# Three of the seven low parts of each residual factor made by GpSimd, in a one-core decoder layer

## The chip, the cores and the metric

The kernel runs on one core of a Trainium2 chip. The metric is the device time of one execution in microseconds; three runs of the kernel before gave 2371.24, 2372.51 and 2374.86 us, and the median, 2372.51 us, is its time. A core has a matrix engine (TensorE, PE in the rows), a vector engine (VectorE, DVE), a scalar engine (ScalarE, ACT), GpSimd (POOL) and SyncE (SP), whose queue issues nearly all transfers here. Each engine works through its own instructions in the order of the program and waits on semaphores where it needs another engine's result.

## The reference

One decoder layer on 512 tokens of width 2048, in float32. What matters here is the three matrix products behind the mixing heads, and what lies between them:

```python
x = x + jnp.concatenate([a_out, r_out], axis=-1) @ w_o[i]
h2 = rms_norm(x, g_ffn[i])
x = x + (jax.nn.silu(h2 @ w_gate[i]) * (h2 @ w_up[i])) @ w_down[i]
gate = jax.nn.sigmoid(rms_norm(x, g_ple[i]) @ w_ple_gate[i] + b_ple_gate[i])
x = x + (p[i] @ w_ple_proj[i]) * gate
```

Twice, a sum with the residual `x` becomes the left side of the next product: after `w_o` (for the gate and up products) and after `w_down` (for `w_ple_gate`). The factor of the norm that belongs to a token is applied behind the product, so the sum can be turned into factors as it comes, 512 columns at a time.

## The kernel before

Every product in float32 precision is made of three matrix products in a rounded format: an operand is split into a high part `H`, its rounded copy made by ScalarE, and a low part `L = source - H`, made by VectorE (`split`, lines 51 to 58). `mm3` multiplies high by high, high by low, low by high.

On top of that, most products run as seven block products in place of eight (a Strassen scheme with 512x512 quarters), named P1 to P7 and run in the order 1, 5, 6, 3, 7, 2, 4. The left side needs seven factors: `a0` and `a1` are two 128x512 chunks of the transposed sum, four of the factors are differences of their halves (`s1` to `s4`), three are halves themselves. `factors` (line 173) makes them: for each product, in that order, the subtraction where there is one, then the split, each on a tile of 128x256:

```python
made = {"1": a0[:, lo], "5": s1, "6": s2, "3": s4, "7": s3, "2": a1[:, lo], "4": a1[:, hi]}
for p in ORDER:
    if p in first:
        first[p]()
    H, L, end = sink(p)
    split(H, L, made[p])
    end()
```

The weights go through the same: each step of a stage (a `Group`: seven products of three or four weight units each) loads a weight tile of 128x1024 (`raw`, line 223), adds a second one to it on VectorE where the product wants a sum (line 81), splits it into `wh` (ScalarE, line 54) and `wl` (VectorE, line 55), and multiplies. `wh` and `wl` have three buffers each.

The sums become factors in `residual` (line 346). When the four token blocks of 512 columns are done, it calls `to_factors` twice (`u` = 0 and 1). TensorE transposes two chunks, ScalarE copies them out of PSUM with the gain of the norm into `a0` and `a1` (tile name `A`), and `factors` follows. There are two groups of columns (`n`), two halves of each (`nh`) and two calls (`u`), so eight calls after `w_o` and eight after `w_down`, in pairs. The buffers that the calls share are few, all from one pool: two for `A`, two for the differences (`t`, of which one holds `s1` and `s2`, the other `s3` and `s4`), four for the factors that are stored to memory first (`o`, line 191; the store is line 194). In the first group of columns all seven factors are stored and loaded again later (`s`, line 206); in the second one they are written straight into the tile `s` that the next stage reads, but for P4 of the first pair. `A` is also the scratch tile of the squares that ScalarE sums for the norm (line 365).

In this part of the program the order on each engine is the outcome of a scheduler that runs over the recorded operations (it reckons when each engine would come to them); TensorE's and the weight loads' program order is not pinned here. SyncE's one queue holds the stores of the factors, the loads of weights and the loads of the old residual, in one line. GpSimd has had little to do: it raises to the power -1/2 (line 84) and issues 16 stores (line 925).

Of the kernel before, what the change touches and what calls it, by code (L numbers as in the profile page):

```python
# [10 lines left out]
F32 = mybir.dt.float32  # L11
# [3 lines left out]
ALU = mybir.AluOpType  # L15
# [18 lines left out]
def layer_kernel(ctx, tc, x, xT, pT, g_mix, wqk, w_vg, qk_norm, g_ret, w_ow, g_ffn,  # L34
                 w_gu, w_dn, g_ple, w_pl, b_pg, w_pp,
                 ident_c, rope_c, ropeT_c, decay_c, mask_c, out):
    nc = tc.nc
# [10 lines left out]
    dram = ctx.enter_context(tc.tile_pool(name="dram", bufs=1, space=bass.MemoryType.DRAM))  # L48


    def split(H, L, src, scale=None):

        if scale is None:
            return (nc.scalar.activation(H, src, AF.Copy),  # L54
                    nc.vector.tensor_tensor(L, src, H.bitcast(F32), op=ALU.subtract))  # L55
        return (nc.scalar.activation(H, src, AF.Copy, scale=scale),
                nc.vector.scalar_tensor_tensor(L, src, scale, H.bitcast(F32),
                                               op0=ALU.mult, op1=ALU.subtract))
# [18 lines left out]
    def sub(o, a, b):  # L77
        nc.vector.tensor_tensor(o, a, b, op=ALU.subtract)  # L78
# [91 lines left out]
    def ev_tile(tag, bufs=2, shape=(P, T), name=None, dt=F32):  # L170
        return pools["ev"].tile(list(shape), dt, name=name or tag, tag=tag, bufs=bufs)

    def factors(a0, a1, sink):

        lo, hi = slice(0, 256), slice(256, 512)
        t = [ev_tile("t", 2, (P, 2, 256)) for _ in range(2)]
        s1, s2, s3, s4 = t[0][:, 0], t[0][:, 1], t[1][:, 0], t[1][:, 1]
        made = {"1": a0[:, lo], "5": s1, "6": s2, "3": s4, "7": s3, "2": a1[:, lo], "4": a1[:, hi]}
        first = {"5": lambda: sub(s1, a0[:, hi], a1[:, hi]), "6": lambda: sub(s2, a0[:, lo], s1),
                 "3": lambda: sub(s4, a1[:, lo], s2), "7": lambda: sub(s3, a1[:, hi], s2)}  # L180
        for p in ORDER:
            if p in first:
                first[p]()
            H, L, end = sink(p)
            split(H, L, made[p])
            end()

    def into(tiles, k):
# [22 lines left out]
    class Group:  # L211
# [36 lines left out]
        def extract(self, p, u):  # L248
            wh = wq.tile([P, 2, T], F32R, name="wh", tag="wh")
            wl = wq.tile([P, 2, T], F32R, name="wl", tag="wl")  # L250
            parts = split(wh, wl, self.raw[SOURCE[p], u])
            self.w[p, u] = wh, wl
            if p == "4":
                self.load_next("11", u)
            elif p == "7":
                self.load_next("12", u)
            self.ready(p, u)
            return parts
# [67 lines left out]
    def chunk_of(get, k):  # L326

        tp = tp_p.tile([P, T], F32, name="tp", tag="tp")
        for b in range(NB):
            transpose(tp[:, b * P:(b + 1) * P], get(b)[:, k * P:(k + 1) * P])  # L330
        return tp

    def to_factors(get, k0, sink, gain=None):

        tps = [chunk_of(get, k) for k in (k0, k0 + 1)]
        a1 = ev_tile("A")
        if gain is None:
            nc.scalar.activation(a1, tps[1], AF.Copy)
            factors(tps[0], a1, sink)
        else:  # L340
            a0 = ev_tile("A")
            nc.scalar.activation(a0, tps[0], AF.Copy, scale=gain(k0))
            nc.scalar.activation(a1, tps[1], AF.Copy, scale=gain(k0 + 1))
            factors(a0, a1, sink)

    def residual(n, i, units, old, new, turn):

# [7 lines left out]
        def finish(th, nh, b, part, t):  # L355
            tb = 2 * th + b
            s = 2 * n + nh
            o = t if (th, nh) == (0, 0) else part
            plus(o, part, t)
            later(1, lambda: nc.sync.dma_start(new(tb, s), o))  # L360
            if turn is None:
                return
            j, gain, where, tiles = turn
            sq = ev_tile("A", name="sq")
            nc.scalar.activation(sq, o, AF.Square, accum_out=ssq[j][:, tb, s:s + 1])
            outs[tb, nh] = o
            if len([k for k in outs if k[1] == nh]) < NB:
                return
            for u in range(2):
                k = 4 * n + 2 * nh + u  # L370
                sink = spill(where, k)
                if n == 1:
                    direct = into(tiles, k)
                    sink = (lambda p, a=spill(where, k - 2), b=direct: a(p) if p == "4" else b(p)) if nh else direct
                wait = 1 + 2 * u if n == 0 else units - 2 + u if nh else 1 + u
                later(wait, lambda u=u, sink=sink: to_factors(
                    lambda b: outs[b, nh], 2 * u, sink, lambda c: gain[:, 4 * s + c:4 * s + c + 1]))
            if n == 1 and nh == 0:
                rstd_of(ssq[j], rstd[j])
                if j == 2:  # L380
                    nc.vector.tensor_scalar(minus, rstd[j], -1.0, None, op0=ALU.mult)
# [30 lines left out]
    class Plain:  # L412
# [16 lines left out]
        def extract(self, p, u):  # L429
            self.w[u] = [wq.tile([P, 2, T], F32R, name=n, tag=n) for n in ("wh", "wl")]  # L430
            if u:
                return split(*self.w[u], self.raw[u])
            for c in range(2):
                split(*(w[:, c] for w in self.w[u]), self.raw[u][:, c])
# [426 lines left out]
    def mixed(i, made):  # L861
        spilled = spill(s_mix, i, 0)
        direct = into(s_o, i)
        assert (not s_o) == (i < 2 * NPAIR - 2)
        factors(*made, lambda p: (direct if p in s_o else spilled)(p))
# [98 lines left out]
    def swiglu(j):  # L964
        kg = min(j // 4, 2)
        act = {}

        def finish(th, nh, b, part, _):
            tb = 2 * th + b
            if nh == 1:  # L970
                act[tb] = part
                return
            r = rstd[1][:, tb:tb + 1]
            s = ev_tile("g", 4) if th == 0 else part
            nc.scalar.activation(s, part, AF.Silu, scale=r)
            a = act[tb]
            nc.vector.scalar_tensor_tensor(a, a, r, s, op0=ALU.mult, op1=ALU.mult)
            if tb == 3:
                for u in range(2):
                    sink = spill(s_a[kg], 2 * (j - 4 * kg) + u)  # L980
                    later(1 + 2 * u, lambda u=u, sink=sink: to_factors(lambda b: act[b], 2 * u, sink))
        return evacuate(finish)
# [132 lines left out]
```

## Time and profile before

| | |
|---|---|
| median of three runs | 2372.51 us (2371.24 to 2374.86) |
| the profiled execution | 2372.15 us, its span 2370.3 us |
| TensorE matmul busy | 2319.2 us (98%) |
| VectorE busy | 1943.6 us (82%), 2626 instructions |
| ScalarE busy | 1198.1 us (51%) |
| GpSimd busy | 59.0 us (2%), 47 instructions |
| granted TensorE clock, mean | 0.996 of full speed |

The span runs from the first instruction to the last, and 1.85 us of the execution lie outside it. TensorE is busy nearly all the time, so its idle time, some 51 us, and the time in which its clock is below full speed, are what other engines can cost. A busy share tells little by itself: the rows below look at the two places where sums become factors, 790 to 925 us and 2118 to 2236 us of the span. A row of the timeline gives start, duration, engine, line, operation, output and inputs, and in brackets how long the engine had idled before it and what ended that. VectorE's durations overlap a little: an instruction of 1.23 us that is followed at once by another is followed after some 1.14 us.

### The profile page before, as it was taken

The page shows a single profiled execution, that of the slowest core. Times are in us where ns is not written, and L with a number is a line of the kernel's source. Part 1 is how long each engine was busy: PE and PEld are TensorE (multiplying, and loading weights), DVE is VectorE, ACT ScalarE, POOL GpSimd, SP SyncE. Part 2 cuts the span into 40 slices and gives each one's busy share as a digit, 9 for nine tenths or more (in the row PEclk, how much of TensorE's full clock was granted, in tenths as well). Part 3 has the DMA queues.
Part 4 walks back from the last instruction along what each step waited for, and adds up shares of the span by engine and source line. Part 5 has one row for each costly group of instructions (what it writes and reads, how often), then busy time and mean ns, then how long its engine had stood idle before and what let it go on. Part 6 is the DMA issues. An engine that isn't in the chain of part 4 may idle for free.

```text
span 2370.3 us, 29145 instructions
## 1 busy us (share of the span) xinstructions
PE 2319.2 (98%) x10480; PEld 1900.2 (80%) x10480; DVE 1943.6 (82%) x2626; ACT 1198.1 (51%) x1791; POOL 59.0 (2%) x47
## 2 busy tenths in 40 slices
PE   9999999999999999999999999999999999999898
PEld 7888878888877877888888888888878878887677
DVE  8888586766667998888988898888888878789997
ACT  7644454444455565544554455444544434356553
POOL 0000011100010002000000000000000000000000
PEclk9999999999999999999999999999999999999999
DMA  6634734445666694346434643465577756857663
GB/s 237 236 130 162 232 104 127 131 147 179 200 219 259 218 359 153 109 155 200 154 113 146 200 160 120 138 196 166 195 318 253 291 224 214 344 196 268 245 197 124
DMA packets 166096, 463.59 MB, mean 196 GB/s; under 512 B 18496, under 2 KB 31168, under 8 KB 160960
## 3 DMA queue, kind: packets, MB, share of 16 engines
q1 hardware_dynamic: 161968, 453.34, 55.7%
q10 hardware_dynamic: 2704, 4.20, 0.7%
q0 software_dynamic: 1280, 4.20, 0.5%
q8 instruction: 82, 1.34, 0.2%
q14 instruction: 62, 0.51, 0.1%
HBM read 352.09 MB, written 105.38 MB: 193 GB/s over the span
## 4 chain that ended last, share of the span: by engine, by line
PE 72%; DVE 14%; DMA 7%; issue 3%; ACT 3%; POOL 0%; SPq 0%; ACTq 0%; DVEq 0%; POOLq 0%
PE Y L63 26%; PE Z L63 17%; PE X L63 15%; PE acc L63 10%; DVE wl L55 5%; DVE raw L81 3%; PE at L63 3%; DMA raw<-in_w_dn 2%; ACT wh L54 2%; PE tp L68 1%; DMA h<-o 1%; DVE t L78 1%; DMA raw<-in_w_gu 1%; DVE o L55 1%; DVE s L55 1%
## 5 line engine op out<-in xcount | busy, mean ns | idle before, releaser
L54 ACT ACTIVATE wh<-raw 128x1024 fp32r<-128x1024 f32 (+1 forms) x728 | 769.5, 1059 | 857.1 <-PE Y L63 295.5
L55 DVE TENSOR_TENSOR wl<-raw,wh 128x1024 fp32r<-128x1024 f32 (+1 forms) x728 | 887.4, 1223 | 278.2 <-ACT wh L54 277.5
L63 PE MATMUL Y<-wh,s 128*128 128x512 f32 x2160 | 682.6, 391 | 7.1 <-DVE v L78 3.8
L63 PEld LDWEIGHTS Y<-wh,s 128*128 128x128 f32 x2160 | 406.1, 188 | 93.7 <-ACT wh L54 6.5
L63 PE MATMUL Z<-wh,s 128*128 128x512 f32 x1504 | 477.7, 393 | 0.8 <-ACT wh L54 0.7
L81 DVE TENSOR_TENSOR raw<-raw 128x1024 f32<-128x1024 f32 x376 | 455.2, 1223 | 25.5 <-DMA raw<-in_w_gu 8.9
L63 PE MATMUL Y<-wl,s 128*128 128x512 f32 x1080 | 425.2, 394 | 2.0 <-DVE wl L55 2.0
L63 PE MATMUL X<-wh,s 128*128 128x512 f32 x1312 | 414.5, 391 | 4.0 <-ACT pp L924 2.7
L63 PEld LDWEIGHTS Z<-wh,s 128*128 128x128 f32 x1504 | 284.2, 189 | 60.7 <-ACT wh L54 2.5
L63 PE MATMUL Z<-wl,s 128*128 128x512 f32 x752 | 299.7, 398 | 10.0 <-DVE wl L55 9.8
L63 PEld LDWEIGHTS X<-wh,s 128*128 128x128 f32 x1312 | 245.9, 188 | 56.9 <-ACT wh L54 3.5
L63 PE MATMUL X<-wl,s 128*128 128x512 f32 x656 | 256.9, 392 | 2.6 <-DVE wl L55 2.5
L63 PEld LDWEIGHTS Y<-wl,s 128*128 128x128 f32 x1080 | 203.3, 188 | 46.4 <-DVE wl L55 5.2
L63 PEld LDWEIGHTS Z<-wl,s 128*128 128x128 f32 x752 | 142.5, 189 | 45.4 <-DVE wl L55 15.9
L63 PE MATMUL acc<-h,wh 128*128 128x512 f32 x512 | 160.3, 394 | 0.8 <-DVE m L681 0.8
L63 PEld LDWEIGHTS X<-wl,s 128*128 128x128 f32 x656 | 123.2, 188 | 30.4 <-DVE wl L55 5.1
L63 PE MATMUL acc<-wh,h 128*128 128x512 f32 x384 | 130.1, 398 | 1.4 <-DVE m L681 1.1
L63 PEld LDWEIGHTS acc<-h,wh 128*128 128x128 f32 x512 | 92.5, 188 | 17.7 <-issue 1.4
L63 PE MATMUL acc<-h,wl 128*128 128x512 f32 x256 | 100.4, 392 | 0.0
L63 PEld LDWEIGHTS acc<-wh,h 128*128 128x128 f32 x384 | 72.3, 188 | 16.7 <-issue 2.6
L54 ACT ACTIVATE o<-t 128x256 fp32r<-128x256 f32 x146 | 58.1, 412 | 37.5 <-DVE t L78 22.9
L63 PE MATMUL acc<-wl,h 128*128 128x512 f32 x192 | 75.3, 392 | 0.6 <-DVE wl L55 0.6
(196 smaller groups left out, 2079.8 us busy)
## 6 DMA issues: line engine op xcount, KB each, us to landing
raw<-in_w_gu SPq DMA_DIRECT2D x176, 512.0 KB, 4.3
raw<-in_w_dn SPq DMA_DIRECT2D x88, 512.0 KB, 6.0
a<-o SPq DMA_DIRECT2D x154, 256.0 KB, 2.9
raw<-in_wqk SPq DMA_DIRECT2D x63, 512.0 KB, 3.7
s<-a SPq DMA_DIRECT2D x14, 2048.0 KB, 10.6
raw<-in_w_vg SPq DMA_DIRECT2D x48, 512.0 KB, 5.4
raw<-in_w_ow SPq DMA_DIRECT2D x32, 512.0 KB, 5.1
xin<-x SPq DMA_DIRECT2D x64, 256.0 KB, 5.3
```

Source lines behind the costliest of these rows:

```text
L54: return (nc.scalar.activation(H, src, AF.Copy), nc.vector.tensor_tensor(L, src, H.bitcast(F32), op=ALU.subtract))
L55: nc.vector.tensor_tensor(L, src, H.bitcast(F32), op=ALU.subtract))
L63: ins = nc.tensor.matmul(*args, **kw)
L68: ins = nc.tensor.transpose(o, a, ident)
L78: nc.vector.tensor_tensor(o, a, b, op=ALU.subtract)
L81: nc.vector.tensor_tensor(o, a, b, op=ALU.add)
```

## The change

`factors` gets a flag, and `to_factors` sets it where there is a gain, which is where residual sums become factors. With it, the low parts of P7, P2 and P4 are subtracted by GpSimd in place of VectorE. The other calls of `factors` (the mixing heads and the SwiGLU activations) are as before, and the high parts stay on ScalarE.

```diff
-    def split(H, L, src, scale=None):
+    def split(H, L, src, scale=None, engine=None):
 
         if scale is None:
             return (nc.scalar.activation(H, src, AF.Copy),
-                    nc.vector.tensor_tensor(L, src, H.bitcast(F32), op=ALU.subtract))
+                    (engine or nc.vector).tensor_tensor(L, src, H.bitcast(F32), op=ALU.subtract))
...
-    def factors(a0, a1, sink):
+    def factors(a0, a1, sink, shared=False):
+
...
             H, L, end = sink(p)
-            split(H, L, made[p])
+            split(H, L, made[p], engine=nc.gpsimd if shared and p in "724" else None)
             end()
...
             nc.scalar.activation(a1, tps[1], AF.Copy, scale=gain(k0 + 1))
-            factors(a0, a1, sink)
+            factors(a0, a1, sink, True)
```

The scheduler orders this part anew. VectorE, at the end of the stage of `w_o`, the last pair of calls, before (`s_7610`, `s_7950`, `s_8110`, `s_7631`, `s_7685`, `s_7768` and `s_7855` are the factor tiles of P1, P2, P4, P5, P6, P3 and P7 of the next stage):

```order
L55 TENSOR_TENSOR s_7610<-A,s_7610 128x256
L55 TENSOR_TENSOR s_7855<-t,s_7855 128x256
L81 TENSOR_TENSOR raw<-raw 128x1024
L78 TENSOR_TENSOR t<-A 128x256
L55 TENSOR_TENSOR s_7950<-A,s_7950 128x256
L55 TENSOR_TENSOR s_8110<-A,s_8110 128x256
L81 TENSOR_TENSOR raw<-raw 128x1024
L78 TENSOR_TENSOR t<-A,t 128x256
L55 TENSOR_TENSOR wl<-raw,wh 128x1024
```

and the same place now:

```order
L55 TENSOR_TENSOR s_7685<-t,s_7685 128x256
L55 TENSOR_TENSOR s_7768<-t,s_7768 128x256
L81 TENSOR_TENSOR raw<-raw 128x1024
L78 TENSOR_TENSOR t<-A 128x256
L55 TENSOR_TENSOR s_7610<-A,s_7610 128x256
L81 TENSOR_TENSOR raw<-raw 128x1024
L78 TENSOR_TENSOR t<-A,t 128x256
L55 TENSOR_TENSOR wl<-raw,wh 128x1024
```

The subtractions into `s_7950`, `s_8110` and `s_7855` have left VectorE; the row `t<-A` is the first one there that reads the second call's `A`.

ScalarE at that place now, where line 343 and 344 (342 and 343 before) are the copies into `a0` and `a1`:

```order
L54 ACTIVATE s_7855<-t 128x256
L343 ACTIVATE A<-tp,gf 128x512
L344 ACTIVATE A<-tp,gf 128x512
L54 ACTIVATE s_7610<-A 128x256
L54 ACTIVATE s_7950<-A 128x256
L54 ACTIVATE s_8110<-A 128x256
L54 ACTIVATE wh<-raw 128x1024
```

The second call's copy into `a1` takes the buffer that the first call's P2 and P4 low parts read, and the high part of a weight stands behind it.

GpSimd's queue at the same place now (before, the only row here was the power, `rstd_84`):

```order
L55 TENSOR_TENSOR s_7855<-t,s_7855 128x256
L84 TENSOR_TENSOR rstd_84<-rstd_84,neghalf 128x4
L55 TENSOR_TENSOR s_7950<-A,s_7950 128x256
L55 TENSOR_TENSOR s_8110<-A,s_8110 128x256
L55 TENSOR_TENSOR s_7855<-t,s_7855 128x256
L55 TENSOR_TENSOR s_7950<-A,s_7950 128x256
L55 TENSOR_TENSOR s_8110<-A,s_8110 128x256
L55 TENSOR_TENSOR s_7855<-t,s_7855 128x256
```

The power stands behind the low parts of the pair before and ahead of those of the last pair; after `w_down` it stands at the same place, and there VectorE needs its result at once (`minus`, line 381).

## Rows read from the trace of the kernel before

**Rows 1.** Busy time by stretch: the stretch in us of the span, its length, then busy us (and instructions) of PE, PEld, DVE, ACT and POOL, the granted clock of TensorE, the share of the DMA engines, GB/s.

```profile
796.00:831.00 35.00, 34.84 (x163) 28.64 (x162) 34.64 (x43) 21.01 (x35) 0.00 (x0) 1.00 0.38 122
831.00:880.00 49.00, 49.00 (x226) 40.33 (x225) 44.40 (x69) 32.22 (x58) 0.00 (x0) 1.00 1.00 347
880.00:925.00 45.00, 40.64 (x168) 30.07 (x167) 41.79 (x64) 26.75 (x48) 13.63 (x1) 0.96 0.45 182
2118.00:2165.00 47.00, 42.62 (x199) 34.47 (x198) 44.30 (x64) 30.92 (x53) 0.00 (x0) 1.00 0.60 202
2165.00:2195.00 30.00, 30.00 (x135) 24.64 (x135) 27.14 (x45) 18.62 (x36) 0.00 (x0) 0.95 1.03 366
2195.00:2236.00 41.00, 35.07 (x145) 25.61 (x144) 39.30 (x66) 25.43 (x50) 1.01 (x1) 0.96 0.64 255
925.00:2070.00 1145.00, 1138.66 (x5086) 938.18 (x5085) 964.00 (x1105) 546.39 (x686) 0.00 (x0) 1.00 0.56 194
```

**Rows 2.** Timeline of PE, the long waits: in 880 to 925 us, then in 2135 to 2240 us.

```profile
907.66 0.50 PE L63 MATMUL Z<-wl,s 128*128 128x512 f32 x1 [1.73 <-DVE wl L55]
...
2164.37 0.62 PE L63 MATMUL Y<-wh,s 128*128 128x512 f32 x1 [3.75 <-DVE v L78]
...
2205.44 0.71 PE L63 MATMUL Z<-wl,s 128*128 128x512 f32 x1 [2.00 <-DVE wl L55]
```

**Rows 3.** Groups of DVE's low parts by shape, with count, busy us and mean ns: those of 880 to 925 us, of 2118 to 2165 us, and of 2195 to 2236 us.

```profile
L55 DVE TENSOR_TENSOR s<-t,s 128x256 fp32r<-128x256 f32 x12 | 4.9, 432 | 0.0
L55 DVE TENSOR_TENSOR s<-A,s 128x256 fp32r<-128x256 f32 x8 | 3.1, 429 | 0.0
L55 DVE TENSOR_TENSOR o<-A,o 128x256 fp32r<-128x256 f32 x1 | 0.4, 419 | 0.0
...
L55 DVE TENSOR_TENSOR o<-t,o 128x256 fp32r<-128x256 f32 x11 | 4.5, 425 | 0.0
L55 DVE TENSOR_TENSOR o<-A,o 128x256 fp32r<-128x256 f32 x7 | 3.0, 427 | 0.0
...
L55 DVE TENSOR_TENSOR s<-t,s 128x256 fp32r<-128x256 f32 x15 | 6.0, 428 | 0.0
L55 DVE TENSOR_TENSOR s<-A,s 128x256 fp32r<-128x256 f32 x8 | 3.2, 424 | 0.0
L55 DVE TENSOR_TENSOR o<-A,o 128x256 fp32r<-128x256 f32 x1 | 0.4, 429 | 0.0
```

**Rows 4.** Timeline of GpSimd's power of 128x4 after `w_o`, and of DVE beside it, from where it starts to where it ends (rows between left out).

```profile
898.00 13.63 POOL L84 TENSOR_TENSOR rstd<-rstd,neghalf 128x4 f32<-128x4 f32 x1 [164.00 <-DVE rstd L89]
...
897.74 0.17 DVE L89 TENSOR_SCALAR rstd<-rstd 128x4 f32<-128x4 f32 x1
897.81 0.43 DVE L78 TENSOR_TENSOR t<-A,t 128x256 f32<-128x256 f32 x1
898.15 1.23 DVE L55 TENSOR_TENSOR wl<-raw,wh 128x1024 fp32r<-128x1024 f32 x1
...
901.09 1.10 DVE L55 TENSOR_TENSOR s<-t,s 128x256 fp32r<-128x256 f32 x3
...
909.98 0.78 DVE L55 TENSOR_TENSOR s<-t,s 128x256 fp32r<-128x256 f32 x2
911.27 2.36 DVE L55 TENSOR_TENSOR wl<-raw,wh 128x1024 fp32r<-128x1024 f32 x2 [0.51 <-ACT wh L54]
```

**Rows 5.** The same power elsewhere: two at which DVE reads PSUM or idles, then two behind each other at 402 us with DVE's rows beside them.

```profile
336.98 1.01 POOL L84 TENSOR_TENSOR rs<-ms,neghalf 128x4 f32<-128x4 f32 x1 [24.48 <-DVE ms L689]
...
336.80 0.69 DVE L678 TENSOR_TENSOR z<-acc,rope 128x512 f32<-128x512 f32 x1
...
2212.10 1.01 POOL L84 TENSOR_TENSOR rstd<-rstd,neghalf 128x4 f32<-128x4 f32 x1 [1300.47 <-DVE rstd L89]
...
2212.45 1.23 DVE L55 TENSOR_TENSOR wl<-raw,wh 128x1024 fp32r<-128x1024 f32 x1 [0.42 <-ACT wh L54]
...
402.43 2.76 POOL L84 TENSOR_TENSOR rs<-ms,neghalf 128x4 f32<-128x4 f32 x1 [3.43 <-DVE ms L689]
...
405.17 2.02 POOL L84 TENSOR_TENSOR rs<-ms,neghalf 128x4 f32<-128x4 f32 x1
...
403.63 0.69 DVE L81 TENSOR_TENSOR z<-z,m 128x512 f32<-128x512 f32 x1
404.23 0.23 DVE L689 TENSOR_SCALAR ms<-ms,eps 128x4 f32<-128x4 f32 x1
...
405.10 1.23 DVE L55 TENSOR_TENSOR wl<-raw,wh 128x1024 fp32r<-128x1024 f32 x1
406.61 0.30 DVE L727 TENSOR_TENSOR at<-at,sides 128x128 f32<-128x128 f32 x1 [0.29 <-PE at L63]
```

**Rows 6.** Busy us of DVE (and its instructions), granted clock and DMA in three stretches between its openings.

```profile
803.20:830.70 27.50, 27.50 (x35) 1.00 0.37 113
...
2128.60:2152.90 24.30, 24.30 (x34) 1.00 0.40 122
2213.80:2232.60 18.80, 18.77 (x32) 1.00 0.37 137
```

**Rows 7.** ScalarE's copies into `a1`, 790 to 930 us; and who SP's queue waited for, 2110 to 2240 us (us in total, times, longest).

```profile
L343 ACT ACTIVATE A<-tp,gf 128x512 f32<-128x512 f32 x8 | 5.4, 676 | 0.0
...
SPq L194 <- DVE o L55: 24.6, 12, 6.3
```

## The prediction, made before the changed kernel ran

> **What bounds the kernel.** I read the busy times by stretch first [rows 1]. Between 925 and 2070 us TensorE works 1138.66 of 1145 us while VectorE works 964: there TensorE is the bound, and nothing the change does reaches it. The two places where sums become factors look different. VectorE is busy 34.64 of 35 us in the first stretch, 41.79 of 45 in the third, 44.30 of 47 in the fourth, 39.30 of 41 in the last. TensorE loses time in three of them: 45 - 40.64 = 4.36 us, 47 - 42.62 = 4.38 us, 41 - 35.07 = 5.93 us, together 14.67 us. The same rows give a granted clock of 0.96 in the third and the last and 0.95 in the fifth: 0.04 x 45 + 0.05 x 30 + 0.04 x 41 = 4.9 us more. So some 19.6 us is all that a lighter VectorE could win here.
>
> Next, who TensorE waits for there [rows 2]: VectorE's low parts of weights (1.73 and 2.00 us) and a sum of VectorE's (3.75 us). VectorE is the bound of the three stretches, and its time is what the change must be priced in.
>
> **What the change removes.** 16 calls x 3 low parts = 48 subtractions leave VectorE. Three of one kind in a row take 1.10 us, the last of them some 0.43, so one costs (1.10 - 0.43) / 2 = 0.335 us from start to start [rows 4]; 48 x 0.335 = 16.1 us. Only those in the three waiting stretches count. There stand 21, 18 and 24 low parts [rows 3], of which three in seven go: 9, 8 and 10, together 27, or 27 x 0.335 = 9.0 us.
>
> **What it adds.** 48 subtractions of 128x256 on GpSimd. The trace has no such row. The nearest are its powers of 128x4: 1.01 us where nothing is in the way [rows 5], 13.63 us in the worst place [rows 4]. A wider tile must take longer, but a subtraction may be simpler than a power, so the lower bound is VectorE's own 0.335 us, the upper one the 13.63 us. I take 1.3 us for the work itself, an estimate: 1.01 us for the power alone, plus the 0.25 us by which VectorE's 128x256 rows (0.42 us) exceed its 128x4 row (0.17 us) [rows 3, 4].
>
> [...]
>
> The longer term is when GpSimd may work. Its power after `w_o` lasts 13.63 us, from 898.00 to 911.63 [rows 4]. All that time up to about 910.7 us VectorE runs one subtraction or addition after another, each with both inputs in SBUF; at 911.27 it shows its first idle time, 0.51 us, and the power ends some 0.9 us after that gap begins. At 402 us it is the same on a small scale: the first power ends 0.95 us after VectorE came to an operation with one input tile (404.23), the next 0.95 us after a weight's low part ended (405.10 + 1.14) [rows 5]. Where VectorE reads PSUM (336.80) or idles (2212.1), the power takes 1.01 us at once. So GpSimd gets its inputs only where VectorE leaves an opening: a gap, or an operation that takes at most one input from SBUF. The saturated stretches have few: VectorE is busy 27.5 of 27.5 us, 24.3 of 24.3 and 18.77 of 18.8 [rows 6].
>
> [...]
>
> **What is queued behind.** A low part that has to wait holds its buffers. The second call of a pair copies into the `A` that the first call's P2 and P4 low parts still read, and into the `t` that its P7 low part reads. ScalarE waits at that copy, in the order shown with a weight's high part behind it; VectorE comes to its `t<-A`, which needs the copy, and stands. That is the opening, and GpSimd works off its queue. So I count one forced stop for a pair of calls: two low parts at 1.3 us and the copy, 0.68 us [rows 7], 3.3 us. Before, VectorE did the six low parts of the pair itself in 6 x 0.335 = 2.0 us. The pair costs 1.3 us more than it saves. Of the eight pairs, 27 / 6 = 4.5 fall into the waiting stretches: 4.5 x 1.3 = 5.9 us. The other 3.5 pairs fall where TensorE is fully fed and cost nothing, VectorE's idle time (4.6 us in the second stretch, 2.9 in the fifth [rows 1]) hides them; without that cover they would cost 4.6 us.
>
> Two waits are left out of this sum and kept for the range. GpSimd's power after `w_down` now stands behind six low parts, and VectorE needs its result (`minus`) two instructions later: up to 6 x 1.3 = 7.8 us of standing, if none of the six found an opening. And SyncE's queue holds the stores of P7, P2 and P4, with weight loads behind them. It already waits 24.6 us, 12 times, for low parts of VectorE after `w_down` [rows 7]; the 3.75 us wait of TensorE at 2164 us is what such a late load costs now [rows 2]. There are four pairs whose factors are stored: at worst 4 x 3.75 = 15 us.
>
> No other instruction changes its engine. The scheduler moves weight splits and additions by a few places; I take that at nothing, since the sum of VectorE's work is what binds, between -3 and +3 us (one weight step of VectorE either way).
>
> **Sum.** 2372.15 us for the profiled execution + 5.9 = 2378.0 us. The profiled execution is 0.36 us below the median of the runs, which I leave.
>
> **The rivals.**
>
> *The openings suffice (faster).* VectorE's load falls by 9.0 us in the waiting stretches, and as it runs ahead it waits for ScalarE more often, which makes openings by itself. GpSimd has far more time than work there, and P7, P2 and P4 are the last three factors that the next stage reads, so that lateness alone harms nobody. Then TensorE's 14.67 us of waits shrink by 9.0, and the clock's 4.9 us by the same share, 3.0: 2372.15 - 12.0 = 2360.2 us. Against it: the buffers above, two `A` and two `t`, allow little lateness.
>
> *Give and take (no change).* GpSimd finds half of its openings and the forced stops take what the low parts gave: 0 +- 4 us, 2372 us. This is also what a GpSimd operation of half my price gives. For it speaks that the sum is a small difference of two uncertain terms.
>
> *GpSimd holds VectorE back (much slower).* A low part that has begun on GpSimd may in turn stop VectorE's next two-input operation until it is done. [...] At 2212.10 the power began, and VectorE's low part of a weight, at 2212.45, still took its 1.23 us [rows 5]; but the power reads four columns, a low part reads 256. If each of the 27 holds VectorE for 1.01 us, the price is 27 x 1.01 - 9.0 = 18.3 us: 2390.5 us. It decides as soon as a hold is longer than 0.335 us. Late stores in SyncE's queue would give about the same time.
>
> **How the numbers follow.** Chances: forced stops 0.37, openings suffice 0.25, give and take 0.25, held back 0.13. The forecast is the first, 2378.0 us; its own range is 2373 to 2387 (between no stop in half of the pairs and the wait at `minus` besides). The whole range reaches to the openings' case on one side and just past the held one on the other, 2361 to 2392, and leaves out some 2 in 10. A measurement of this kernel can tell about 0.2%, 4.7 us, from no change. Faster by more: 0.25 of the openings, plus 0.02, less 0.01: 0.26. Slower by more: 0.30 of the forced stops' 0.37, 0.13 held back, 0.02 of give and take: 0.45. The same: the remaining 0.29.
>
> **What would show it.** Steps in the changed profile: 48 rows of 128x256 on GpSimd, many of them far longer than 1.3 us and ending just after an opening of VectorE; ScalarE's copies into `A` (now line 344) and VectorE's `t<-A` waiting for GpSimd; TensorE's lost time in the three stretches longer by about 6 us. If GpSimd's rows are near 1 us, or they are long and nobody waits for them, the forecast is wrong to the fast side. If VectorE's instructions grow longer beside GpSimd's, or start late without a releaser, the third rival holds. If the weights' loads land late in the pairs that store, the queue was the price.

## The result and the profile after

The changed kernel takes 2391.18 us (median of 4 runs, 2389.78 to 2392.67); the kernel before, run beside it, 2373.07 us (4 runs). The ratio is 1.0071, with a 95% interval of 1.0059 to 1.0082: slower by 0.7%. The forecast was 2378.0 us, with a range of 2361 to 2392. The direction and the range held. The size did not: 18.1 us where the sum had 5.9. The time stands where the rival "GpSimd holds VectorE back" put it, at 2390.5.

The page of the profile after, with busy us, share of the span and instructions of each engine:

```profile
PE 2326.0 (97%) x10480; PEld 1903.1 (80%) x10480; DVE 1941.0 (81%) x2578; ACT 1198.6 (50%) x1791; POOL 109.2 (5%) x95
```

To find where the time went, both traces are cut at the same instructions: from ScalarE's first `e<-Z` of `w_o` to the first SiLU on the product of the next stage (the place after `w_o`), and between two `e<-Z` around the place after `w_down`. The busy times by stretch, in the columns of [rows 1], of before:

```profile
751.82:958.70 206.88, 202.36 (x902) 163.42 (x901) 181.00 (x241) 117.02 (x187) 13.63 (x1) 0.99 0.72 256
2081.93:2306.57 224.64, 212.66 (x928) 170.33 (x927) 205.61 (x278) 126.39 (x199) 1.01 (x1) 0.98 0.68 234
```

and of after:

```profile
753.64:973.28 219.64, 205.22 (x902) 165.78 (x901) 179.58 (x217) 117.45 (x186) 36.06 (x25) 0.97 0.67 242
2096.81:2323.66 226.85, 212.92 (x927) 169.23 (x926) 203.59 (x253) 125.59 (x199) 28.86 (x25) 0.98 0.67 232
```

The place after `w_o` is 12.8 us longer, the place after `w_down` 2.2 us. (The rest of the 17.7 us between the spans is 1.8 us ahead of the first mark, where the change reaches nothing, and 0.9 us elsewhere. In the runs below this lead differs by up to 5.6 us, so places are compared from mark to mark.) In the first place TensorE's idle time grows from 206.88 - 202.36 = 4.5 us to 14.4, and the same 902 matmuls take 2.9 us more at a lower granted clock, 0.97 against 0.99. VectorE has 24 instructions less there, 24 x 0.335 = 8.0 us, yet is busy only 1.4 us less: 179.58 against 181.00.

The groups of GpSimd's instructions (columns as in [rows 3], then what ended the idle time before them) are new; only the last was there before, as in [rows 4]:

```profile
L55 POOL TENSOR_TENSOR o<-t,o 128x256 fp32r<-128x256 f32 x8 | 21.8, 2724 | 1347.2 <-ACT o L54 1347.2
L55 POOL TENSOR_TENSOR o<-A,o 128x256 fp32r<-128x256 f32 x20 | 20.3, 1018 | 8.0 <-ACT o L54 7.9
L55 POOL TENSOR_TENSOR s<-A,s 128x256 fp32r<-128x256 f32 x12 | 13.2, 1111 | 33.5 <-ACT s L54 23.3 <-PE Y L63 9.7 <-DMA xin<-x 0.5
L55 POOL TENSOR_TENSOR s<-t,s 128x256 fp32r<-128x256 f32 x8 | 8.1, 1011 | 25.8 <-ACT s L54 25.8
L84 POOL TENSOR_TENSOR rstd<-rstd,neghalf 128x4 f32<-128x4 f32 x3 | 3.0, 1011 | 130.5 <-DVE rstd L89 130.5
```

Most low parts take about 1 us. The P7 low parts of stored calls, first in their call, take 2.7 us on average. The timeline shows what the longest does (GpSimd, then SyncE's queue, ScalarE, VectorE, TensorE; the bracket is the wait before a row):

```profile
824.52 5.83 POOL L55 TENSOR_TENSOR o<-t,o 128x256 fp32r<-128x256 f32 x1 [14.50 <-ACT o L54]
...
813.80 20.24 SPq L195 DMA_DIRECT2D h<-o  x8
838.52 0.33 SPq L224 DMA_DIRECT2D raw<-in_w_ow  x1
...
832.82 0.42 ACT L54 ACTIVATE o<-A 128x256 fp32r<-128x256 f32 x1 [5.58 <-DMA h<-o]
...
833.27 0.42 DVE L55 TENSOR_TENSOR o<-A,o 128x256 fp32r<-128x256 f32 x1 [3.51 <-ACT o L54]
...
833.87 0.33 PE L68 MATMUL tp<-ident,xin 128*128 128x128 f32 x1 [2.06 <-ACT A L344]
```

The low part takes 5.83 us, where the quickest take 0.72. Its store is late, the tile `o` is free late, ScalarE stands 5.58 us before the next high part, and VectorE and TensorE stand behind it. The first load of `w_o` behind these stores is issued at 838.52, 84.9 us after the mark; before it was 78.6 us (830.40). Some 55 us later a load of the next weights (`in_w_gu`) is late for ScalarE, and TensorE waits 4.58 us. This trace does not show whether that load is late because of the earlier stand at `o`; the experiments come back to it. In the 10 us in which the wait of 4.58 us ends, and in the 10 us in which one of 2.52 us ends, TensorE's granted clock is 0.66 (0.50 in each single us from 892 to 897 and from 922 to 926):

```profile
891.94 1.06 ACT L54 ACTIVATE wh<-raw 128x1024 fp32r<-128x1024 f32 x1 [2.34 <-DMA raw<-in_w_gu]
...
893.05 1.22 PE L63 MATMUL X<-wh,s 128*128 128x512 f32 x2 [4.58 <-ACT wh L54]
921.88 0.80 PE L63 MATMUL Z<-wl,s 128*128 128x512 f32 x1 [2.52 <-DVE wl L55]
...
890.00:900.00 10.00, 6.91 (x21) 5.12 (x22) 6.93 (x7) 3.17 (x3) 0.40 (x1) 0.66 1.04 418
920.00:930.00 10.00, 8.12 (x23) 6.44 (x24) 9.08 (x13) 3.95 (x6) 1.87 (x1) 0.66 0.00 0
```

Where TensorE's long wait in this region was 1.73 us before [rows 2], it now waits 4.58 and 2.52. And VectorE's rows beside GpSimd's are longer than their kind:

```profile
807.67 1.75 DVE L55 TENSOR_TENSOR wl<-raw,wh 128x1024 fp32r<-128x1024 f32 x1
811.10 1.21 DVE L55 TENSOR_TENSOR wl<-raw,wh 128x1024 fp32r<-128x1024 f32 x1
```

The first of these two ran while GpSimd worked; it is 0.54 us longer.

### The profile page after: what moved, and what is told of

Read it like the earlier page. It is cut to its first block, busy times and chain, and to the rows that moved or that the text cites. A ratio compares the mean times of both kernels' runs of the same rounds, so it can differ in the third digit from the quotient of the medians.

```text
span 2388.0 us, 29212 instructions
## 1 busy us (share of the span) xinstructions
PE 2326.0 (97%) x10480; PEld 1903.1 (80%) x10480; DVE 1941.0 (81%) x2578; ACT 1198.6 (50%) x1791; POOL 109.2 (5%) x95
## 4 chain that ended last, share of the span: by engine, by line
PE 45%; DMA 8%; DVE 7%; issue 2%; ACT 2%; POOL 0%; SPq 0%; DVEq 0%; ACTq 0%; POOLq 0%
PE Y L63 19%; PE Z L63 13%; PE X L63 12%; DVE wl L55 3%; DMA raw<-in_w_gu 2%; DVE raw L81 2%; DMA raw<-in_w_dn 1%; DMA s<-a 1%; DMA h<-o 1%; ACT wh L54 1%; PE tp L68 1%; DMA pp<-pp 1%; DVE t L78 1%; DMA xin<-x 0%; DVE e L81 0%
## 5 line engine op out<-in xcount | busy, mean ns | idle before, releaser
L63 PEld LDWEIGHTS acc<-h,wh 128*128 128x128 f32 x512 | 92.4, 188 | 17.7 <-issue 1.4
L55 POOL TENSOR_TENSOR o<-t,o 128x256 fp32r<-128x256 f32 x8 | 21.8, 2724 | 1347.2 <-ACT o L54 1347.2
```

The source lines that it names most:

```text
L55: (engine or nc.vector).tensor_tensor(L, src, H.bitcast(F32), op=ALU.subtract))
L63: ins = nc.tensor.matmul(*args, **kw)
```

## The experiments

Three theories. *Contention*: GpSimd's reading and VectorE's get in each other's way, so GpSimd starves (the 5.83 us) and VectorE is held (the 1.75 us instead of 1.21). *Order*: the scheduler's new order of instructions, SyncE's queue above all, loads late. *Lateness*: results that come late hold the few tiles `o`, `A` and `t` and the stores. In the table, us are (ratio - 1) x 2373; the places are from one profile each, as the difference to before's 206.88 and 224.64. The scheduler orders each kernel anew, so where it matters the text says whose order a kernel has (the orders are those in which the traces show the instructions and transfers). "Own queue" means that the stores of all seven factors go by GpSimd's queue.

| kernel | ratio (95%) | us | after `w_o` | after `w_down` |
|---|---|---|---|---|
| the change | 1.0071 (1.0059 to 1.0082) | +16.8 | +12.8 | +2.2 |
| write only | 1.0014 (1.0005 to 1.0024) | +3.3 | +5.8 | -2.5 |
| idle work | 1.0029 (1.0016 to 1.0041) | +6.9 | +5.1 | +1.8 |
| first place only | 1.0055 (1.0038 to 1.0071) | +13.1 | +12.3 | +0.8 |
| three stores on GpSimd's queue | 1.0064 (1.0049 to 1.0079) | +15.2 | +11.7 | +2.9 |
| write only, own queue | 0.9981 (0.9971 to 0.9990) | -4.5 | +3.1 | -5.9 |
| before, own queue | 1.0029 (1.0019 to 1.0038) | +6.9 | +3.8 | +2.8 |
| the change, own queue | 1.0055 (1.0039 to 1.0071) | +13.1 | +11.9 | +4.5 |
| direct calls only | 1.0014 (1.0005 to 1.0024) | +3.3 | +5.0 | +0.2 |
| stored calls only | 1.0060 (1.0043 to 1.0078) | +14.2 | +10.7 | +3.1 |
| one input | 1.0022 (1.0012 to 1.0032) | +5.2 | +6.5 | -2.0 |

### GpSimd writes and reads nothing

```diff
+        if engine is not None:
+            high = nc.scalar.activation(H, src, AF.Copy)
+            low = engine.memset(L.bitcast(F32), 0.0)
+            paced(low, high)
+            return high, low
```

> The changed kernel, but GpSimd fills the 48 low parts of P7, P2 and P4 with zeros, each after its high part, instead of computing them: it writes the same tiles at the same places and reads nothing (the low parts of these three products are left out of the result). If the price is GpSimd's reading beside VectorE (GpSimd starved, VectorE held), VectorE keeps the relief and nobody waits long: 2360 to 2373 us, faster than or equal to before (2373). If the price is the scheduler's new order of instructions, or the mere fact that another engine with its own semaphores makes these parts, it stays: 2388 to 2392 us, like the changed kernel (2391).

Measured: 2377.24 us, +3.3. Between the two, and nearer to contention: reading costs 1.0071 - 1.0014 = 0.0057, 13.5 us of the 16.8. The order differs little between the two (after `w_o`, all but one of SyncE's 113 transfers and 205 of VectorE's 216 instructions come in the same order). Its stretches:

```profile
752.98:965.61 212.63, 202.47 (x901) 163.41 (x901) 173.17 (x217) 117.51 (x187) 8.48 (x25) 0.99 0.70 250
2090.15:2312.27 222.12, 209.95 (x929) 168.82 (x928) 197.15 (x252) 125.12 (x198) 8.59 (x25) 0.98 0.69 237
```

Here VectorE has its relief: 173.17 us in the first place, 7.8 less than before. In after it has 179.58 with the same 217 instructions, so reading by GpSimd lengthened VectorE's work there by 6.4 us (203.59 - 197.15 = 6.4 in the second place, too). But even with the relief the first place is 5.8 us longer than before: something else ate it, and GpSimd's reading is not it.

### Work on GpSimd that nobody waits for

In the kernel before. Its trace shows the other engines in before's order, one for one in both places:

```diff
...
+            twice = ident[:, None, :].to_broadcast([P, 2, P])
+            paced(nc.gpsimd.tensor_tensor(unread, twice, twice, op=ALU.subtract), high)
```

> The kernel before, with VectorE making all low parts, and 48 more subtractions of 128x256 on GpSimd, one after the high part of each factor of P7, P2 and P4, on a constant, into a tile that nobody reads. The order on VectorE, ScalarE, TensorE and SyncE is that of before. If GpSimd's reading holds VectorE by about 0.54 us each (as after's rows suggest: 1.75 us for a weight's low part instead of 1.21), the 27 in the waiting stretches cost 27 x 0.54 = 14.6 us: about 2387 us, at least 2380. If a GpSimd operation that nobody waits for does not hold VectorE, and the price is lateness through the few buffers and SyncE's queue, it is 2373 us within 3.

Measured: 2381.34 us, +6.9: over the bound of 2380, half of what was priced. VectorE, with before's 241 instructions, is busy 187.13 us in the first place instead of 181.00:

```profile
757.43:969.42 211.99, 202.19 (x902) 161.87 (x901) 187.13 (x241) 117.36 (x187) 52.27 (x25) 1.00 0.70 251
2092.25:2318.68 226.43, 211.31 (x926) 168.56 (x925) 207.15 (x276) 126.64 (x198) 64.13 (x25) 0.98 0.68 232
```

In the second place it is held for only 207.15 - 205.61 = 1.5 us, while GpSimd's rows there add up to 64.13 us. With the order unchanged, VectorE's 6.1 + 1.5 = 7.6 us more cost 6.9 us. The durations of the 48 (ns: shortest, median, longest) and the row of VectorE at which the longest, begun before 2140 us, ended:

```profile
L57 POOL TENSOR_TENSOR unread<-ident x48: 607/1252/24212, 809.1 to 2249.9; 128x256 bf16<-128x256 f32 x48
...
2163.36 1.23 DVE L61 TENSOR_TENSOR wl<-raw,wh 128x1024 fp32r<-128x1024 f32 x1 [0.36 <-ACT wh L60]
```

One subtraction lasted 24.2 us, in which VectorE ran 32 operations, and ended at VectorE's first idle time since. So both happen: GpSimd starves, and it holds VectorE.

### One place only

Here `shared` is true after `w_o` (`j == 1`) and false after `w_down`.

```diff
-            factors(a0, a1, sink, True)
+            factors(a0, a1, sink, shared)
```

> The changed kernel with GpSimd making low parts in the first place only (the 24 after w_o); the place after w_down is as before. By the marker at the first product of the next stage, after loses 14.6 us in the first place of 17.7 in all. If the two places add up, about 2387 us (2385 to 2389). If the loss comes with the order of the whole program, which the scheduler makes anew, it may be anything between 2375 and 2391.

Measured: 2387.11 us, as the sum by places said (its 14.6 us take in the 1.8 us ahead of the mark). The place after `w_down`, in which VectorE makes all low parts as before, stands at +0.8.

### The stores of P7, P2 and P4 on GpSimd's queue

```diff
-            store = lambda: nc.sync.dma_start(where[p][:, k].bitcast(F32), o.bitcast(F32))
+            queue = nc.gpsimd if own and p in "724" else nc.sync
+            store = lambda: queue.dma_start(where[p][:, k].bitcast(F32), o.bitcast(F32))
...
-                sink = spill(where, k)
+                sink = spill(where, k, own=True)
```

> The changed kernel, but the stores of the factors of P7, P2 and P4 (4 pairs of calls, 24 stores) go out by GpSimd's own queue behind its low parts, so that SyncE's queue, with the weight loads, waits for no GpSimd low part. If late stores in SyncE's queue are the larger part of the price (TensorE waits of about 4.8 us at 810 to 860 and 5.1 us at 880 to 930 begin behind them), 2378 to 2384 us. If the price is VectorE held back by GpSimd's reading, or lateness through the tiles A and t, 2388 to 2394 us; writing DMA descriptors on GpSimd may then make it a little later still.

Measured: 2390.0 us, within the interval of the change. With these stores gone from SyncE's queue, ScalarE stands at `o` for 8.1 us in all, the longest time 3.2 us, and the price stays. So neither the stand at `o` nor GpSimd's low parts in SyncE's queue has been shown to be the price. They are not ruled out by this run alone, since a move of stores has a price of its own (the next runs: 6.9 us in the kernel before), and issuing one takes GpSimd 0.56 us on average.

### Reading or not, with all factor stores on GpSimd's queue

The same with all seven products' stores, in three kernels that differ in who makes the 48 and in whether GpSimd reads.

```diff
+            store = lambda: (nc.gpsimd if own else nc.sync).dma_start(where[p][:, k].bitcast(F32), o.bitcast(F32))
...
```

> The write-only kernel (GpSimd fills the 48 low parts with zeros, which are left out of the result), and the stores of all seven factors go out by GpSimd's own queue, so that SyncE's queue has no factor store ahead of a weight load. The write-only kernel took 2377.2 us although VectorE had 48 subtractions less and GpSimd read nothing; SyncE's new order puts seven more stores ahead of the first late load of w_o. If that order is what ate the relief, the time falls to 2366 to 2372 us. If something else did (VectorE's and ScalarE's new order, or the waits on another engine), it stays at 2375 to 2380 us.

> The kernel before with all low parts on VectorE and the stores of the seven factors of the stored calls on GpSimd's queue: the control to the run beside it. If stores in SyncE's queue hold up weight loads already before (it waits 23.8 us for VectorE's low parts between 785 and 862 us), it is faster than before: 2366 to 2371 us. If those loads are early enough, 2371 to 2376 us. Were it as much faster as its partner, the relief of VectorE would be worth nothing.

> The changed kernel, with GpSimd computing the 48 low parts, and the stores of all seven factors of the stored calls by GpSimd's queue: the partner of the write-only kernel with the same stores (2369.8 us) and of the kernel before with the same stores (2382.0). The three differ in nothing but who makes the 48 and whether GpSimd reads. If the contention for reading (starved, then holding VectorE) costs about what it costs with SyncE's stores (2391.2 - 2377.2 = 14 us), 2381 to 2386 us. If that price was mostly SyncE's queue behind starved low parts, 2370 to 2376 us.

Measured: 2369.83 us for writing only, as the first statement had it; 2381.96 for VectorE making all, where both statements said less; 2388.54 for GpSimd computing, just above the 2381 to 2386 for contention. The three are not alike in all but the reading, as the third text has it: the second has an order near to before's, the first and the third have one near to the change's.

Between the first two, relieving VectorE of the 48 is worth 0.0048, 11.4 us, with the other order in it; that is close to the 12.0 of the rival "the openings suffice". Between the first and the third, GpSimd's reading costs 0.0074, 17.6 us. Taking the stores off SyncE's queue gives the write-only kernel 7.8 us back, gives the change 3.8 us (within the intervals), and makes the kernel before 6.9 us slower. So the relief exists: writing only, with its own queue, is the one kernel that is faster than before. In the write-only kernel with SyncE's stores the new order ate it. That this went by way of SyncE's queue is suggested by the 7.8 us and not shown, since the same move costs the kernel before time. There, in the write-only kernel, three stores and a reload of a factor stand between the first two loads of the next weights, where before there was one store: the second load is issued at 854.89, 101.9 us after the mark, instead of 96.1 (847.90). What else in the order costs was not taken apart. The first places, write only and then computing:

```profile
754.27:964.23 209.96, 201.62 (x902) 163.28 (x901) 173.19 (x217) 117.29 (x186) 24.59 (x55) 0.99 0.69 253
```

```profile
751.89:970.63 218.74, 204.21 (x902) 165.71 (x901) 179.89 (x217) 117.67 (x187) 44.67 (x55) 0.96 0.66 243
```

With the same 217 instructions VectorE is busy 6.7 us longer, and TensorE's idle time is 14.5 us instead of 8.3.

These runs also answer for the chain through `o`. Where ScalarE's high parts wait for a store to give `o` back (785 to 960 us: us in total, times, longest), before, writing only with SyncE's stores, and computing with its own queue:

```profile
ACT o L54 <- DMA h<-o: 10.1, 7, 2.6
ACT o L54 <- DMA h<-o: 10.9, 5, 6.6
ACT o L54 <- DMA h<-o: 10.4, 4, 3.7
```

and in the last of these the first load of `w_o`, and TensorE's wait for the next weights:

```profile
831.59 6.16 SPq L224 DMA_DIRECT2D raw<-in_w_ow  x2
...
PE X L63 <- ACT wh L54: 7.6, 1, 7.6
```

Writing only has a longer stand at `o` than the change, 6.6 us against 5.6, and costs 3.3 us. Computing with its own queue has stands like before's and its first load of `w_o` 79.7 us after the mark, 1.1 us later than before, and yet its first place is 11.9 us longer: there TensorE waits 7.6 us at the load of the next weights, where the change waits 4.58. The move of the stores alone costs the kernel before 3.8 us in this place. So some 12.8 - (11.9 - 3.8) = 4.7 us of the change's 12.8 may have gone through `o`, an estimate, and most of the price is there without it. What makes the load of the next weights late was not found.

### Direct calls or stored calls

The flag `shared` set for n = 1 alone, then for n = 0 alone.

> The changed kernel with GpSimd making low parts only in the calls of n = 1 (whose factors stay in SBUF but for two), 24 of the 48. If the price begins with the late stores of the first pairs and the late loads at 880 us are only its consequence, 2371 to 2377 us. If it stands in both halves alike, some 2382 us.

> The other 24: GpSimd makes low parts only in the calls of n = 0, whose factors are stored to DRAM. If the price begins with the stored pairs (GpSimd starved for 5.83 us with a full VectorE, ScalarE and VectorE behind it, loads 8 us late), 2384 to 2390 us. If it stands in both halves alike, some 2382 us.

Measured: 2378.02, just above its range, and 2389.44 us: +3.3 and +14.2. Their sum, 17.5, is the change's 16.8 within the intervals. The price comes with the stored calls. The first places, direct and then stored:

```profile
754.61:966.48 211.87, 203.77 (x902) 164.50 (x901) 182.47 (x229) 117.01 (x187) 16.02 (x13) 0.98 0.71 251
```

```profile
754.98:972.58 217.60, 205.47 (x901) 165.79 (x901) 179.81 (x229) 117.89 (x186) 23.78 (x13) 0.97 0.67 244
...
825.88 5.83 POOL L55 TENSOR_TENSOR o<-t,o 128x256 fp32r<-128x256 f32 x1 [14.50 <-ACT o L54]
...
834.18 0.42 ACT L54 ACTIVATE o<-A 128x256 fp32r<-128x256 f32 x1 [5.56 <-DMA h<-o]
```

Both have 12 instructions less on VectorE than before, which leaves 181.00 - 12 x 0.335 = 177.0 us. So the direct calls hold VectorE for 5.5 us there and the stored ones for 2.8: the cheap half is the one that holds VectorE more. Between these two kernels the time does not go by VectorE's lost time. They differ in their order as well: after `w_o` SyncE issues all 113 transfers in before's order with the direct calls, and in the change's order with the stored ones, and the other engines are close to the same two orders. So this split divides the order as well as the calls. The stored half shows the 5.56 us for which ScalarE stands at `o`, as the change does, but the runs with their own queue speak against that as the larger part of the price. More tiles `o`, and stored calls in which GpSimd only writes, were not tried.

### One input instead of two

```diff
...
+            low = engine.tensor_copy(L, src)
...
```

> The changed kernel, but GpSimd copies the factor into the 48 low parts instead of subtracting (they then hold the factor itself, not its low part): it reads one tile instead of two. If any reading of GpSimd's must wait for an opening of VectorE, 2386 to 2391 us, with copies of several us. If only two-input operations do, 2375 to 2380 us as in the write-only kernel (2377.2), with no GpSimd row above 1 us.

Measured: 2379.67 us, +5.2, within the interval of write only. Both statements on it missed in one half: the time is that of write only, but copies are long too:

```profile
L55 POOL CAST o<-t 128x256 fp32r<-128x256 f32 x8 | 17.5, 2188 | 1348.4 <-ACT o L54 1341.0 <-DMA h<-o 7.4
...
753.34:966.72 213.38, 203.49 (x902) 163.74 (x901) 175.61 (x217) 117.36 (x186) 22.02 (x25) 0.98 0.68 249
```

Copies hold VectorE less (175.61 - 173.17 = 2.4 us in the first place, against 6.4). A copy waits for its turn as well, 2.2 us on average at P7, against 2.7.

### Side by side, without the layer

> No part of the layer: ten blocks, one after the other, of a run of VectorE operations beside a run of GpSimd operations, each released by one instruction of ScalarE. GpSimd alone: 8 subtractions of 128x256 with two inputs, 8 copies, 8 fills. VectorE alone: 12 subtractions of 128x1024 with both inputs in SBUF. Then these 12 beside GpSimd's 8 subtractions, 8 copies, 8 fills; 16 VectorE subtractions with one input in PSUM beside the 8; 12 VectorE operations with one input beside the 8; 24 of 128x256 with both inputs in SBUF beside the 8. If GpSimd's reading and VectorE's with two SBUF inputs exclude each other: alone 0.72 to 0.74 us each as in after; beside the 12, one GpSimd subtraction of several us, and each that gets its turn lengthens VectorE's run by some 0.54 us; beside a VectorE operation that reads PSUM, 0.73 us and nothing lost on either side; fills undisturbed everywhere. If the holds in after came from somewhere else (DMA traffic, ScalarE), both engines keep their durations of alone in all blocks.

The rows of a block are VectorE's run (start, us, count) and GpSimd's; first GpSimd's 8 subtractions alone and VectorE's 12 alone, then VectorE's 12 beside the 8 subtractions and beside 8 fills, and last GpSimd's row beside the 12:

```profile
10.87 6.34 POOL L62 TENSOR_TENSOR g<-s,u 128x256 f32<-128x256 f32 x8 [10.43 <-ACT tok L39]
...
24.61 15.08 DVE L58 TENSOR_TENSOR d<-a,b 128x1024 f32<-128x1024 f32 x12 [24.61 <-ACT tok L39]
39.97 18.30 DVE L58 TENSOR_TENSOR d<-a,b 128x1024 f32<-128x1024 f32 x12 [0.27 <-ACT tok L39]
...
74.61 15.08 DVE L58 TENSOR_TENSOR d<-a,b 128x1024 f32<-128x1024 f32 x12 [0.33 <-ACT tok L39]
...
40.01 13.40 POOL L62 TENSOR_TENSOR g<-s,u 128x256 f32<-128x256 f32 x8 [15.67 <-ACT tok L39]
```

A GpSimd low part costs 6.34 / 8 = 0.79 us alone and 1.68 beside VectorE, which loses 3.22 / 8 = 0.40 for each; beside fills VectorE loses nothing. There is no subtraction of several us: the expected starving did not show. VectorE's operations wrote one tile there and followed each other more slowly than in the layer (15.08 / 12 = 1.26 us against 1.13), so a second run gave them four tiles in turn.

> No part of the layer: blocks as in the first side-by-side run, but VectorE's operations write four tiles in turn, as in the layer, instead of one and the same. There 12 of 128x1024 took 15.08 us alone, 1.257 us each, and GpSimd's 8 subtractions came through beside them in 13.40 us, VectorE 3.22 us longer; in the layer such operations follow each other every 1.13 us. If the gap between them is the opening that GpSimd uses, then here the 12 take some 13.7 us alone, and beside GpSimd's 4 subtractions 13.7 us too, while the first of the 4 lasts until the 12 are done (some 13 us, as the power of 13.63 us did before). If GpSimd gets its turn in any case, it is as in the first run: VectorE longer by some 0.4 us for each of the 4, GpSimd done in 7 us. The three other forms are also run alone, so that it can be said what each loses: one input in PSUM nothing (16 in 11.5 us), one input in SBUF nothing (12 in 11.9 us), 24 of 128x256 with both in SBUF alone some 8.1 us (0.335 each).

Here a row is one VectorE instruction: two with two inputs beside GpSimd's 4 subtractions, one after these are done, one beside the 4 copies, then one with an input in PSUM beside 8 subtractions, and one with a single input, alone and beside them:

```profile
26.69 1.22 DVE L65 TENSOR_TENSOR e<-a,b 128x1024 f32<-128x1024 f32 x1 [0.27 <-ACT tok L40]
27.83 1.74 DVE L65 TENSOR_TENSOR d<-a,b 128x1024 f32<-128x1024 f32 x1
...
34.49 1.21 DVE L65 TENSOR_TENSOR d<-a,b 128x1024 f32<-128x1024 f32 x1
...
45.33 1.41 DVE L65 TENSOR_TENSOR e<-a,b 128x1024 f32<-128x1024 f32 x1
...
68.81 0.68 DVE L67 TENSOR_TENSOR e<-a,bank 128x512 f32<-128x512 f32 x1
...
78.20 0.69 DVE L68 TENSOR_SCALAR d<-a 128x1024 f32<-128x1024 f32 x1
...
86.92 1.21 DVE L68 TENSOR_SCALAR e<-a 128x1024 f32<-128x1024 f32 x1
...
26.74 6.75 POOL L69 TENSOR_TENSOR g<-s,u 128x256 f32<-128x256 f32 x4 [26.30 <-ACT tok L40]
```

VectorE's operations follow each other every 1.13 us, as in the layer, and still GpSimd gets its turn after each: the 4 subtractions lengthen the second to the fifth VectorE row from 1.22 to 1.74 us, 0.52 each, and are done in 6.75 us. A copy costs the neighbour 0.2 us (1.41 against 1.21), an operation that reads PSUM loses nothing (0.68 us alone, too), one with a single input goes from 0.69 to 1.21, and one of 128x256 with two inputs from 0.42 to 0.94 (0.94 stands in the change's trace as well, at 917.41 us beside a subtraction of GpSimd's). So the hold is settled, at 0.52 us for each subtraction that gets in between two operations. In the layer not all do: 6.4 / 0.52 is some 12 of the 24 in a place, an estimate, and the copies' 2.4 / 0.2 is 12 as well. The gap between operations is not what lets GpSimd in, and why it starves in the layer stays open.

## Why the direction was right and the size wrong

That the direction came out is in part luck. The forced stops, of which the forecast's sum is made, are small; the time was lost to holds, which stood in a rival, and to the new order, which stood at nothing. The range held by 0.8 us, and only because it had been stretched to the rival's time; the forced stops' own range ended at 2387.

**VectorE's load is the bound, relief is worth something: right.** The forecast's rival put 9 us of waits and 3 of the clock on it, 12.0 us; the pair with the stores on GpSimd's queue gives 11.4, with a change of order in it. In the second place the write-only kernel is faster than before, too. And where the order is the same or nearly so, the time follows VectorE's: 7.6 us more of its busy time cost 6.9 us (idle work against before), and 6.4 + 6.4 = 12.8 cost 13.5 (the change against write only). The copies, in an order less alike, cost VectorE 2.4 + 2.5 = 4.9 us and the kernel 1.9, against write only.

**The step that failed is the price of a pair, 2 x 1.3 + 0.68 against 2.0 us saved.** It let GpSimd work in forced stops only and let VectorE keep its six low parts' time. A low part alone costs 0.79 us (0.72 in its quickest rows of after), not 1.3. GpSimd does not always need an opening: in the plain runs it got its turn after every operation (4 subtractions in 6.75 us). Nor is an operation with a single input always an opening, as the forecast had it (0.69 to 1.21 us beside a subtraction). And VectorE does not keep its time: of 8.0 us in the first place it keeps 1.4, because a subtraction that gets in between two of its operations holds the next one by 0.52 us, more than the 0.335 us it saves. The rival with the hold named this mechanism. It priced a hold at 1.01 us, twice too much, and counted 27 of them; over the 24 subtractions of a place the mean is 6.4 / 24 = 0.27 us, under its point of decision, 0.335. By holds alone the change would not be slower, so its 2390.5 is nearly right for a reason only half its own. That VectorE is held is now shown: 1.74 us against 1.22, with no loss for the PSUM form (0.68 us alone and beside subtractions) and none beside fills (15.08 us for 12 operations, alone and beside them). And GpSimd's own wait can be for far more than one operation: VectorE ran 32 in its 24.2 us.

**The stops are there, and small at `A`.** ScalarE waits for GpSimd's readers of `A` for 3.3 us in all after `w_o`:

```profile
ACT o L54 <- DMA h<-o: 15.2, 5, 5.6
ACT A L344 <- POOL o L55: 2.2, 2, 1.8
ACT A L343 <- POOL s L55: 1.1, 1, 1.1
```

The forecast looked at `A` and `t`. The longest stands are at `o`, with four buffers that are given back by a store: 15.2 us of waits, the longest 5.6, against 10.1 and 2.6 before.

**Late stores and loads: left out of the sum, and not shown to be the miss.** They stood in the text as "at worst 4 x 3.75 = 15 us", kept for the range. The stored calls cost 14.2 us and the direct ones 3.3, and in the change's trace a chain runs from a starved low part through `o` and SyncE's queue to late loads. But with all these stores on GpSimd's queue the stands at `o` are about as short as before's and most of the price stays, and in the write-only kernel, with a longer stand than the change's, it is 3.3 us.

**Order of instructions at 0 +- 3 us: wrong, and as large a miss as the holds.** With a GpSimd that reads nothing, in nearly the change's order, the time is +3.3 us, where the relief alone would give some -11: about 14 us, an estimate. The first place shows it by VectorE's idle time. It is 25 to 30 us in the four kernels in which VectorE makes the low parts of the stored calls itself (before: 206.88 - 181.00 = 25.9), and 37 to 40 us in the eight in which GpSimd makes them, whether it reads two tiles, one or none, and whichever queue stores them (the change: 219.64 - 179.58 = 40.1). These eight have the new order, or one near it. The order itself and the fact that another engine makes the stored low parts were never taken apart, so which of the two it is stays open.

**The wait at `minus`, up to 7.8 us: did not come.** The power found its turn at once, 1.01 us each time, after `w_o` too, where before it took 13.63 us [rows 4].

## What to carry to other kernels

An idle GpSimd is not free help for a full VectorE: price each operation moved at what it takes from VectorE's neighbour (0.52 us for a 128x256 subtraction with two inputs that gets in between) against what VectorE saves (0.335), and move rather what reads one tile (a copy took 0.2 us from the neighbour) or nothing (a fill took none), or runs beside PSUM readers (0.68 us alone and beside a subtraction). Where a scheduler orders the program anew, the new order is a term of the sum: here it cost as much as the contention. A long wait in one trace is a suspect and not yet the price: the stand at `o` was there without the price, and most of the price without the stand. And to tell contention from order and lateness, give the helper the same work without reading, and the same reading without a reader.

## What the runs showed of the hardware

- A GpSimd subtraction of 128x256 that gets its turn holds one VectorE operation by 0.52 us, at both sizes tried (1.22 to 1.74 us for 128x1024 and 0.42 to 0.94 for 128x256 with two inputs; 0.69 to 1.21 for 128x1024 with one input in SBUF). A copy holds it by 0.2 us (1.21 to 1.41), a fill not at all (12 operations in 15.08 us alone and beside fills), and an operation that reads PSUM is not held (0.68 us alone and beside subtractions). The one-input case was not expected.
- In the layer a GpSimd operation can stand until VectorE has a gap: 5.83 us in the change, 13.63 before, 24.2 us with idle work. Beside 12 operations in the plain runs it never did (8 subtractions in 13.40 us, 4 in 6.75). What tells the two apart was not found.
